# Moving the second gated unit's weights in the load order and issuing three GELU preparations at 1.25 steps a piece

## The chip, the cores and the metric

The kernel runs on one core of one Trainium2 chip. The metric is the device time of one execution in microseconds (us), the median of the runs shown. The core's engines each take their instructions in the order of the program: TensorE (PE, with its weight loads as PEld), VectorE (DVE), ScalarE (ACT), GpSimd (POOL), and SyncE (SP), which here only issues DMAs. ACT issues DMAs too, in the same order as its other instructions; the profile lists these as ACTq and those of SP as SPq.

## The reference

One layer of a bidirectional encoder over 2048 tokens of width 1024, in float32: an RMSNorm, one wide input projection, windowed attention (branch A), a state-space model (branch B), and then, which is the part that matters here:

```python
y = jax.nn.gelu(y)                                    # y: output of the state-space model
y = y * jax.nn.sigmoid(y @ w_glu + b_glu)             # the gated unit (GLU)
ssm = y * jax.nn.silu(z_ssm)
merged = jax.nn.sigmoid(g_attn) * (attn @ w_branch_attn) \
       + jax.nn.sigmoid(g_ssm) * (ssm @ w_branch_ssm)
x = x + merged @ w_out
return rms_norm(x, final_norm_gain)
```

## The kernel before

Float32 accuracy is had from pairs: each operand is split into a rounded part (a copy on ACT, names ending in h) and the rest (a subtraction, names ending in l), and each product is three matmuls: high by high, high by low, low by high.

The tokens are four blocks of 512, worked in the order 2, 3, 1, 0. Everything up to the attention is done first; beside its last projections runs a chain of side work that ends with the GELU of block 2. The final stage is then, for each block: the gated unit `glu` (four pieces of 12 matmuls), `branch` (16 pieces of 12 matmuls), and `outp` (eight groups of 24 matmuls). While `branch` of one block runs, `gelu_prep` of the next block is issued beside it; then comes the next block's `glu`, then `outp` of the first. This text calls them branches 1 to 4; branches 1 to 3 have a GELU beside them.

Instructions go out in the order of the program, written by hand. `turn()` gives each side generator a credit of half its rate, and takes one step of it for each whole credit, while the credit is above zero. In `branch` there are two turns in each piece: one in the middle of the matmuls (`mm3`, after k = 1), and one at the end, in `tick()`. The pieces, counted from 0, are (e, n) = (0,0), (1,0), (0,1), (1,1), (2,0), (2,1), (3,0), (3,1) and so on to (7,1); n = 0 is the attention side and n = 1 the state-space side. A piece issues its matmuls; then a DVE product with the gate (L1543, which frees the PSUM bank); where n = 1 also the sum `m` (DVE, L1547), its copy `mh` (ACT, L1548) and the loads of two gates (ACT's queue, L1500); then `tick()`, which issues the rest `ml` (DVE, L1556) and takes its turn; and last, where n = 0, `wahead(2)`, which splits the weights for two column blocks further: `wh` on ACT (L163), and `wl` on POOL in four quarters (L155). (After the piece (1,0) it is `wahead(1)`, and after (0,1) `wahead(2)`.)

`gelu_prep` has 16 steps. Step 1 issues the loads of the first two 128-row tiles of `yt` (ACT's queue, L1423; each reads runs of 64 floats), step 2 nothing. A tile then takes four sub-steps in four consecutive steps of a sequence that starts every third step: g0 (ACT, L1429), g1 and g2 (DVE L1433, ACT L1437), g3 with the copy `gh` (DVE L1441, ACT L1442), and g4, the rest `gl` (DVE, L1446):

```python
            for k in range(13):
                for s_ in range(3, -1, -1):
                    e, r = divmod(k - s_, 3)
                    if r == 0 and 0 <= e < 4:
                        steps[s_](e)
                yield
                if k in (4, 7):
                    ld((k - 4) // 3 + 2)
```

So step 3 has g0 of tile 0; step 8 the load of tile 2 and g3 of tile 1; step 9 g0 of tile 2; step 11 the load of tile 3 and g3 of tile 2; step 12 g0 of tile 3; steps 13 and 14 g1, g2 and then g3 of tile 3; and step 15 its `gl`.

The weights come through two buffers `raw` (512 KB each, loads on SP), in the order of the list `witems`: item j + 2 is loaded when item j is split and its buffer is free. Between the last projections and the first branch the list holds the output matrix's first half in four quarters (`wo`, split by ACT and DVE), the two `w_glu` items (the first split by ACT and DVE, the second by ACT and POOL), and then the eight items of the branch. In the last three projections of block 1, two items each are split ahead of the matmuls.

Of the kernel before, what the change touches and what calls it, by code (L numbers as in the profile page):

```python
# [37 lines left out]
def kernel(  # L38
# [89 lines left out]
    def add_side(gen, rate=1.0):  # L128
        sd = {"gen": gen, "rate": rate, "credit": 0.0, "done": False}
        sides.append(sd)  # L130
        return sd
# [4 lines left out]
    def drain(sd):  # L136
        while not sd["done"]:
            tick()
# [28 lines left out]
    witems = []  # L167
# [20 lines left out]
    def wsplit_next():  # L188
        j = wpos["split"]
        wload_to(j)  # L190
        it = witems[j]
        if it[0] == "h":
            h_split(it[1], it[2], wraw.pop(j).rearrange("p k c -> p (k c)").rearrange("p (k c) -> p k c", k=2))
        elif it[0] == "wo":
            wo_split(0, it[1], wraw.pop(j).rearrange("p k c -> p (k c)").rearrange("p (k c) -> p k c", k=2), V)
        else:
            wsplit.append(split_w(j, KD, 128, eng=V if j == wpos["glu"] else Q))
        wpos["split"] += 1
        if wpos["lag"]:
            later(wpos["lag"], lambda: wload_to(j + 2))  # L200
        else:
            wload_to(j + 2)
# [86 lines left out]
    def proj(kind, e, b, w):  # L289
        pt = bank("pj")  # L290
        mm3(pt, w, hblk[b], KD)
        evac(kind, e, b, pt)
# [953 lines left out]
    with tc.manual_schedule():  # L1246
# [3 lines left out]
        BO = (2, 3, 1, 0)  # L1250
        wo = {}
# [40 lines left out]
        for b in BO:  # L1292
            for e in (0, 2):
                if b == BO[0]:
                    witems.append(("wo", e))
                    witems.append(("wo", e + 4))
                witems.append([w_glu[0, :, (e + i) * 128:(e + i + 1) * 128] for i in range(2)])
            for e in range(KD):
                witems.append([w[0, :, e * 128:(e + 1) * 128] for w in (w_branch_attn, w_branch_ssm)])
        xp = s1.enter_context(tc.tile_pool(name="xp", bufs=1))  # L1300
# [31 lines left out]
        for b in range(NBLK):  # L1332
            gen = None
            for i, key in enumerate(wlist):
# [20 lines left out]
                if b == 0 and i == 0:  # L1355
                    sg = start(xp, wlist[0:2], wsplit1, wt)
# [47 lines left out]
        def ftile(shape, dt, tag, name, bufs=1):  # L1404
            return fin["fp"].tile(shape, dt, tag=tag, name=name, bufs=bufs)
# [9 lines left out]
        def gelu_prep(b, lag):  # L1415
            gx[b] = [ftile([128, 4, BLK], F32R, t, t) for t in ("gh", "gl")]
            gh, gl = gx[b]
            tl = {}

            def ld(e):  # L1420
                t = ftile([128, D], F32, "xr", "yt", 3)
                y = t[:, 0:BLK].rearrange("p (j m) -> p j m", j=T)
                A.dma_start(out=y, in_=yS[e * 128:(e + 1) * 128, :, b * 64:(b + 1) * 64])  # L1423
                ta = t[:, BLK:D]
                tl[e] = (y.rearrange("p j m -> p m j"), ta, ta.rearrange("p (m j) -> p m j", j=T))

            def g0(e):
                yv, ta, tav = tl[e]
                A.activation(tav, yv, AF.Square, scale=GELU_Q)  # L1429

            def g1(e):
                yv, ta, tav = tl[e]
                V.scalar_tensor_tensor(tav, tav, 1.0, yv, ALU.add, ALU.mult)  # L1433

            def g2(e):
                yv, ta, tav = tl[e]
                A.activation(ta, ta, AF.Tanh, scale=GC)  # L1437

            def g3(e):
                yv, ta, tav = tl[e]  # L1440
                V.scalar_tensor_tensor(tav, tav, 1.0, yv, ALU.add, ALU.mult)  # L1441
                A.activation(gh[:, e], ta, AF.Copy)  # L1442

            def g4(e):
                yv, ta, tav = tl.pop(e)
                V.tensor_tensor(gl[:, e], ta, gh[:, e].bitcast(F32), ALU.subtract)  # L1446

            def g12(e):
                g1(e)
                g2(e)  # L1450

            steps = (g0, g12, g3, g4)
            ld(0)
            ld(1)
            for _ in range(1 + lag):
# [10 lines that stand above are left out]
        def attn_prep(b, lag):  # L1466
            ax[b] = [ftile([128, 4, BLK], F32R, t, t) for t in ("ah", "al")]
            ah, al = ax[b]
            tok = slice(b * BLK, (b + 1) * BLK)
            ar = {}  # L1470

            def ld(e):
                ar[e] = gtile("ar")
                A.dma_start(out=ar[e], in_=aS[e * 128:(e + 1) * 128, tok])

            ld(0)
            ld(1)
            for _ in range(1 + lag):
                yield
            for e in range(4):  # L1480
                if lag:
                    yield
                r = ar.pop(e)
                A.activation(ah[:, e], r, AF.Copy)
                V.tensor_tensor(al[:, e], r, ah[:, e].bitcast(F32), ALU.subtract)
                yield
                if e + 2 < 4:
                    ld(e + 2)
# [14 lines left out]
        def glu(b):  # L1503
            gh, gl = gx.pop(b)
            sx[b] = [ftile([128, 4, BLK], F32R, t, t) for t in ("sh", "sl")]
            sh, sl = sx[b]
            for e in range(4):
                if e + 2 < 4:
                    load_zs(b, e + 2)
                if e % 2 == 0:  # L1510
                    w2 = wnext()
                w = [t[:, (e % 2) * 4:(e % 2) * 4 + 4] for t in w2]
                pt = bank("pj")
                mm3(pt, w, (gh, gl), 4)
                ta = ttile("ta")
                zs = zst.pop((b, e))
                g2 = ftile([128, BLK], F32, "g2", "g2")
                V.tensor_tensor(g2, gh[:, e].bitcast(F32), gl[:, e].bitcast(F32), ALU.add)
                A.activation(ta, pt, AF.Tanh, scale=0.25, bias=fin["bgl"][:, e:e + 1])
                V.tensor_tensor(g2, g2, zs, ALU.mult)  # L1520
                V.scalar_tensor_tensor(ta, ta, 1.0, g2, ALU.add, ALU.mult)
                A.activation(sh[:, e], ta, AF.Copy, scale=0.125)
                V.scalar_tensor_tensor(sl[:, e], ta, 0.125, sh[:, e].bitcast(F32), ALU.mult, ALU.subtract)
                if e == 2:
                    load_gt(b, 0)
                tick()
                if e < 2:
                    wahead(2 + e)
# [46 lines left out]
        def load_xr(b, t, q=None):  # L1575
            r0 = b * BLK + t * 128
            xrs[b, t] = ftile([128, D], F32, "xr", "xr", 3)
            (q or nc.sync).dma_start(out=xrs[b, t], in_=x[r0:r0 + 128, :])
# [95 lines left out]
        ws = [wnext(1), wnext(1), wnext(0)]  # L1674
        for b in (0, 1):
            for n, (key, w) in enumerate(zip(second[-3:], ws)):
                for _ in range(2 if b == 1 else 0):
                    wsplit_next()
                proj(key[0], key[1], b, w)
        drain(sd)  # L1680
# [3 lines left out]
        for i, b in enumerate(BO):  # L1684
            nxt = BO[i + 1] if i + 1 < NBLK else None
            if nxt is not None:
                sg = add_side(gelu_prep(nxt, 1), 1.0)
            branch(b, nxt)
            if nxt is not None:
                drain(sg)  # L1690
            load_xr(b, 0, A)
            if nxt is not None:
                glu(nxt)
                sa = add_side(attn_prep(nxt, 1), 1.0)
            outp(b, nxt is None)
            if nxt is not None:
                drain(sa)
# [48 lines left out]
```

## Time and profile before

| | |
|---|---|
| median of 3 runs | 1496.83 us (1495.30 to 1497.23) |
| the profiled execution's own time | 1497.58 us |
| its span, first to last instruction | 1495.8 us |
| PE busy | 1411.9 us, 94% of the span |
| DVE, ACT, POOL busy | 1042.3, 659.8, 636.9 us |
| granted TensorE clock, mean | 0.981 of full |

The final stage begins at about 1061 us of the span. A timeline row reads: start, length (both us), engine, line of the program, operation, output from input by the program's names, shapes, count; in brackets the idle time of the engine just before, and what ended it. For a DMA on ACTq or SPq the length is that of the issue alone. In a row of groups the numbers after the shapes are the count, then total busy us and the mean in ns, then the idle time before.

### The profile page before, as it was taken

Reading aid. Unit: us, or ns where it says so; the run is one execution under the profiler, and the core shown is the slowest. Engines: PE = TensorE matmul, PEld = TensorE weight load, DVE = VectorE, ACT = ScalarE, POOL = GpSimd, SP = SyncE. Lnnn points to the kernel's source line nnn. Section 1 sums busy time; section 2 is a strip of 40 time slices with the busy share of each in tenths; the row PEclk is TensorE's granted clock in tenths of the full one; section 3 lists DMA queues with packets and bytes.
Section 4 is the critical chain, followed back from the end, with each engine's and each line's share of the span. In section 5 each row is a group of like instructions: output and inputs, shape, how many; then the busy total and the mean of one; then the engine's idle time right before and its main releaser. Section 6 shows DMA issues by size and latency. Waiting matters only on the chain.

```text
span 1495.8 us, 19697 instructions
## 1 busy us (share of the span) xinstructions
PE 1411.9 (94%) x6933; PEld 1151.1 (77%) x6933; DVE 1042.3 (70%) x1954; ACT 659.8 (44%) x1213; POOL 636.9 (43%) x683
## 2 busy tenths in 40 slices
PE   7999779899999999899999999999989999999998
PEld 6787567777778777788888888888767887878886
DVE  2427977779788788656999998883678376485442
ACT  6432133433534534535666666664444243243211
POOL 5520187758688787732111111113367054153320
PEclk9999989989999999999999999999999999999999
DMA  8543222322332332455233333334676476375441
GB/s 268 156 105 90 64 81 74 99 92 71 119 106 82 116 106 82 149 170 142 86 95 93 96 95 89 99 99 141 201 210 175 140 185 184 117 186 177 129 120 70
DMA packets 240722, 185.47 MB, mean 124 GB/s; under 512 B 57920, under 2 KB 202432, under 8 KB 240624
## 3 DMA queue, kind: packets, MB, share of 16 engines
q10 hardware_dynamic: 118192, 107.89, 24.5%
q1 hardware_dynamic: 122432, 76.34, 17.1%
q8 instruction: 54, 0.88, 0.2%
q14 instruction: 44, 0.36, 0.1%
HBM read 126.56 MB, written 57.62 MB: 123 GB/s over the span
## 4 chain that ended last, share of the span: by engine, by line
PE 45%; DVE 19%; POOL 7%; DMA 6%; issue 6%; ACT 4%; ACTq 1%; POOLq 0%; DVEq 0%; SPq 0%
PE pj L221 8%; PE pj L220 8%; PE pj L222 8%; PE s L1593 4%; PE s L1592 4%; PE s L1594 4%; POOL wl L155 3%; DMA yt<-yS 2%; PE s L1163 2%; DVE Hl L891 2%; PE s L1110 2%; PE s L1147 2%; DVE pl L1152 1%; PE s L858 1%; DVE X L879 1%
## 5 line engine op out<-in xcount | busy, mean ns | idle before, releaser
L155 POOL TENSOR_TENSOR wl<-raw,wh 128x256 fp32r<-128x256 f32 x380 | 352.9, 959 | 575.1 <-ACT wh L163 443.6
L220 PE MATMUL pj<-hh,wh 128*128 128x512 f32 x976 | 390.7, 400 | 0.0
L221 PE MATMUL pj<-hl,wh 128*128 128x512 f32 x976 | 385.2, 395 | 0.0
L222 PE MATMUL pj<-hh,wl 128*128 128x512 f32 x976 | 385.1, 395 | 0.0
L222 PEld LDWEIGHTS pj<-hh,wl 128*128 128x128 f32 x976 | 185.4, 190 | 40.9
L220 PEld LDWEIGHTS pj<-hh,wh 128*128 128x128 f32 x976 | 186.1, 191 | 33.9
L221 PEld LDWEIGHTS pj<-hl,wh 128*128 128x128 f32 x976 | 185.8, 190 | 34.1
L163 ACT ACTIVATE wh<-raw 128x1024 fp32r<-128x1024 f32 x96 | 100.7, 1051 | 22.0 <-issue 4.4
L1592 PE MATMUL s<-woh,mh 128*128 128x512 f32 x256 | 101.3, 396 | 0.0
L1594 PE MATMUL s<-woh,ml 128*128 128x512 f32 x256 | 101.3, 396 | 0.0
L1593 PE MATMUL s<-wol,mh 128*128 128x512 f32 x256 | 101.3, 396 | 0.0
L1127 ACT ACTIVATE p<-p,sml 128x384 f32<-128x384 f32 (+1 forms) x128 | 75.8, 594 | 16.3 <-DVE sml L1123 16.2
L404 ACT ACTIVATE st<-pj,bg 128x512 f32<-128x512 f32 x64 | 43.8, 685 | 77.7 <-PE pj L222 71.6
L1111 DVE CUSTOM_DVE_ANT_0 p<-s,bias 128x384 f32<-128x384 f32 (+1 forms) x128 | 68.2, 534 | 14.1 <-PE s L1110 13.7
L1636 POOL TENSOR_TENSOR sm<-sm,mhalf 128x1 f32<-128x1 f32 x15 | 8.3, 551 | 160.3 <-DVE sm L1635 123.7
L867 DVE TENSOR_TENSOR rt<-X,es 128x1020 f32<-128x1020 f32 x32 | 43.3, 1353 | 38.1 <-issue 14.3
L1152 DVE TENSOR_TENSOR pl<-s,ph 128x512 fp32r<-128x512 f32 x92 | 62.8, 683 | 4.3 <-ACT ph L1150 2.9
L1110 PE MATMUL s<-kst,qs 128*128 128x384 f32 (+1 forms) x256 | 65.7, 339 | 0.0
L1599 DVE TENSOR_TENSOR xr<-xr,s 128x512 f32<-128x512 f32 x32 | 21.9, 684 | 60.0 <-PE s L1594 60.0
L870 DVE TENSOR_TENSOR X<-X,rt 128x510 f32<-128x510 f32 x64 | 62.1, 1009 | 1.1
L891 DVE TENSOR_TENSOR Hl<-X,Hh 64x1024 fp32r<-64x1024 f32 x32 | 46.1, 1440 | 17.5 <-ACT Hh L886 17.0
L1594 PEld LDWEIGHTS s<-woh,ml 128*128 128x128 f32 x256 | 48.1, 188 | 11.7
(307 smaller groups left out, 3046.1 us busy)
## 6 DMA issues: line engine op xcount, KB each, us to landing
raw<-in_w_in_dram SPq DMA_DIRECT2D x59, 512.0 KB
gS<-st ACTq DMA_DIRECT2D x64, 256.0 KB
gt<-gS ACTq DMA_DIRECT2D x64, 256.0 KB
x<-in_x_dram SPq DMA_DIRECT2D x16, 512.0 KB
raw<-in_w_branch_attn_dram SPq DMA_DIRECT2D x32, 256.0 KB
raw<-in_w_branch_ssm_dram SPq DMA_DIRECT2D x32, 256.0 KB
out_dram<-xr ACTq DMA_DIRECT2D x15, 512.0 KB
xr<-in_x_dram SPq DMA_DIRECT2D x12, 512.0 KB
```

The lines of the kernel that those rows point to most:

```text
L155: eng.tensor_tensor(lo[:, ks], r[:, ks], hi[:, ks].bitcast(F32), ALU.subtract)
L163: A.activation(res[0], r, AF.Copy)
L220: PE.matmul(pt, w[0][:, k], r[0][:, k], start=start and k == 0, stop=False)
L221: PE.matmul(pt, w[0][:, k], r[1][:, k], start=False, stop=False)
L222: PE.matmul(pt, w[1][:, k], r[0][:, k], start=False, stop=stop and k == kt - 1)
L891: V.tensor_tensor(H[1][rows], xv, H[0][rows].bitcast(F32), ALU.subtract)
L1110: PE.matmul(pt[:, 0:w], s["qs"][:, h], kst[:, r, kv, k0 * 128:k1 * 128], start=r == 0, stop=r == 1)
L1127: A.activation(p[:, h, 0:w], p[:, h, 0:w], AF.Exp, bias=nm[:, j:j + 1], accum_out=den[:, j:j + 1])
L1152: return lambda: V.tensor_tensor(pl, pt, ph.bitcast(F32), ALU.subtract)
L1592: PE.matmul(pt, mh[k][:, ts_], wo[0, n][:, k], start=k == 0, stop=False)
L1593: PE.matmul(pt, mh[k][:, ts_], wo[1, n][:, k], start=False, stop=False)
L1594: PE.matmul(pt, ml[k][:, ts_], wo[0, n][:, k], start=False, stop=k == KD - 1)
```

## The change

Two edits. The last quarter of the output matrix's first half (`wo` 6) moves behind the second `w_glu` item in the list, and the last projection of block 1 splits one item ahead of its matmuls where it split two; so `wo` 6 is split at the end of the first `glu` piece, ahead of the first branch item. And the side generator of the later GELUs gets a rate of 1.25 where it had 1.0: five steps in eight turns in place of four.

```diff
             for e in (0, 2):
                 if b == BO[0]:
                     witems.append(("wo", e))
-                    witems.append(("wo", e + 4))
+                    if e == 0:
+                        witems.append(("wo", 4))
                 witems.append([w_glu[0, :, (e + i) * 128:(e + i + 1) * 128] for i in range(2)])
+                if b == BO[0] and e == 2:
+                    witems.append(("wo", 6))
...
             for n, (key, w) in enumerate(zip(second[-3:], ws)):
-                for _ in range(2 if b == 1 else 0):
+                for _ in range((2, 2, 1)[n] if b == 1 else 0):
                     wsplit_next()
                 proj(key[0], key[1], b, w)
...
             if nxt is not None:
-                sg = add_side(gelu_prep(nxt, 1), 1.0)
+                sg = add_side(gelu_prep(nxt, 1), 1.25)
             branch(b, nxt)
```

## Rows read from the trace of the kernel before

**Rows 1.** Timeline of PE: the gated-unit waits behind branches 1, 2 and 3.
```profile
1137.32 0.50 PE L221 MATMUL pj<-gl,wh 128*128 128x512 f32 x1 [2.10 <-DVE gl L1446]
...
1241.55 0.50 PE L221 MATMUL pj<-gl,wh 128*128 128x512 f32 x1 [1.54 <-DVE gl L1446]
...
1345.53 0.50 PE L221 MATMUL pj<-gl,wh 128*128 128x512 f32 x1 [1.57 <-DVE gl L1446]
```

**Rows 2.** Windows: length, busy of PE, PEld, DVE, ACT, POOL, then clock, DMA.
```profile
1191.00:1235.90 44.90, 44.90 (x194) 35.84 (x192) 32.03 (x38) 19.43 (x25) 22.35 (x25) 1.00 0.74 176
...
1071.00:1074.00 3.00, 3.00 (x9) 2.33 (x8) 2.00 (x3) 2.21 (x4) 1.78 (x3) 0.50 0.76 263
```

**Rows 3.** Timeline of ACT and its DMA queue (ACTq) in branch 2.
```profile
1193.05 0.53 ACTq L1423 DMA_DIRECT2D yt<-yS  x1
...
1194.35 1.06 ACT L163 ACTIVATE wh<-raw 128x1024 fp32r<-128x1024 f32 x1 [1.05 <-issue]
1198.44 1.14 ACT L1429 ACTIVATE yt<-yt 128x512 f32<-128x512 f32 x1 [3.04 <-DMA yt<-yS]
...
1215.12 0.53 ACTq L1423 DMA_DIRECT2D yt<-yS  x1
...
1219.66 1.16 ACT L1429 ACTIVATE yt<-yt 128x512 f32<-128x512 f32 x1 [0.41 <-DMA yt<-yS]
...
1224.53 0.81 ACTq L1500 DMA_DIRECT2D gt<-gS  x2
1225.38 0.53 ACTq L1423 DMA_DIRECT2D yt<-yS  x1
...
1232.00 1.13 ACT L1429 ACTIVATE yt<-yt 128x512 f32<-128x512 f32 x1 [2.98 <-DMA yt<-yS]
```

**Rows 4.** Groups by line in branch 2: count, busy us, mean ns, idle.
```profile
L1556 DVE SCALAR_TENSOR_TENSOR ml<-m,mh 128x512 fp32r<-128x512 f32 x8 | 8.3, 1032 | 8.3 <-ACT mh L1548 8.3
L1547 DVE TENSOR_TENSOR m<-gt 128x512 f32<-128x512 f32 x8 | 7.9, 987 | 0.3
...
L1543 DVE SCALAR_TENSOR_TENSOR gt<-gt,s 128x512 f32<-128x512 f32 x8 | 5.4, 678 | 0.9 <-PE s L222 0.9
L1433 DVE SCALAR_TENSOR_TENSOR yt<-yt 128x512 f32<-128x512 f32 x4 | 4.9, 1224 | 0.0
L1441 DVE SCALAR_TENSOR_TENSOR yt<-yt 128x512 f32<-128x512 f32 x4 | 4.9, 1222 | 0.2
L1446 DVE TENSOR_TENSOR gl<-yt,gh 128x512 fp32r<-128x512 f32 x4 | 2.7, 685 | 0.3 <-ACT gh L1442 0.3
...
L1548 ACT ACTIVATE mh<-m 128x512 fp32r<-128x512 f32 x8 | 5.1, 632 | 8.9 <-DVE m L1547 8.9
...
L1437 ACT ACTIVATE yt<-yt 128x512 f32<-128x512 f32 x4 | 2.5, 634 | 5.4 <-DVE yt L1433 5.4
L1442 ACT ACTIVATE gh<-yt 128x512 fp32r<-128x512 f32 x4 | 2.5, 632 | 5.5 <-DMA gt<-gS 2.8 <-DVE yt L1441 2.7
```

**Rows 5.** Timeline of ACT: the first `yt` step of branches 1 and 3.
```profile
1093.65 1.14 ACT L1429 ACTIVATE yt<-yt 128x512 f32<-128x512 f32 x1 [5.28 <-DMA yt<-yS]
...
1302.84 1.14 ACT L1429 ACTIVATE yt<-yt 128x512 f32<-128x512 f32 x1 [3.19 <-DMA yt<-yS]
```

**Rows 6.** Timeline of the first gated unit; the DMA row is the chain's.
```profile
1066.11 1.06 ACT L1274 ACTIVATE woh<-raw 128x1024 fp32r<-128x1024 f32 x1 [2.46 <-DMA raw<-in_w_out_dram]
...
1068.46 0.37 SPq L183 DMA_DIRECT2D raw<-in_w_branch_attn_dram  x1
1068.73 0.67 ACT L404 ACTIVATE st<-pj,bg 128x512 f32<-128x512 f32 x1
...
1068.90 3.70 POOL L155 TENSOR_TENSOR wl<-raw,wh 128x256 fp32r<-128x256 f32 x4 [27.41 <-ACT wh L163]
...
1073.05 4.78 DMA raw<-in_w_branch_ssm_dram
...
1073.65 0.67 ACT L1519 ACTIVATE ta<-pj,bgl 128x512 f32<-128x512 f32 x1
```

## The prediction

> **What bounds the kernel now.** I read the waits of PE first, then the timeline of PE, ACT and DVE through the final stage, then groups by line for the prices. PE is the bound: in branch 2 it is busy in all 44.9 us at full clock [rows 2], which makes 44.9 / 16 = 2.8 us a piece. Its waits come where the next block's gated unit begins: the eleventh matmul of its first piece waits for `gl` of the GELU's last tile, 2.10, 1.54 and 1.57 us behind branches 1, 2 and 3 [rows 1]. The rows of branch 3 stand 104.0 us behind those of branch 2 [rows 1]; 20 pieces of 2.8 and eight groups of 24 matmuls of 2.8 / 12 each make 100.8, so a round holds some 3.2 us of waits, and no change of the GELU's order can win more there. Ten matmuls are 2.33 us, so without that last wait each gated unit would have begun at 1135.0, 1239.2 and 1343.2. I compare these three marks, because behind them PE runs on.
>
> The reader is to see a second thing: ACT, in program order, stands still at g0 until `yt` has landed, 3.04 us for tile 0 and 2.98 us for tile 3 [rows 3]. From issue to the step it took 5.39 us (tile 0), 4.54 (tile 2) and 6.62 (tile 3) [rows 3]. Whatever lies behind g0 on ACT waits too.
>
> **The change, the GELU's rate.** Credits rise by 0.625 a turn instead of 0.5. With m for a piece's middle and e for its end, steps 1 to 15 stood at m0, m1, ... m14. Now they stand at m0, e0, e1, m2, m3, m4, e4, e5, m6, m7, m8, e8, e9, m10, m11. No instruction is added or removed; the order on ACT and DVE changes, and with it what is behind a wait:
>
> - g0 of tile 0 (step 3) was behind the weight split `wh` for piece 4 (1194.35, then 1198.44) [rows 3]; at e1 it comes ahead of it.
> - g0 of tile 2 (step 9) moves from m8 to m6, ahead of the split for piece 10; its load (step 8) is now half a piece ahead of it, not a whole one, and only a `gh` lies between them on ACT.
> - g0 of tile 3 (step 12) moves from m11 to e8, ahead of the split for piece 12, again half a piece behind its load.
> - `gh` of tile 3 (step 14) moves to m10, ahead of the split for piece 14.
>
> So three loads that used to hold up little now stand before the weights that PE needs next. The question is whether the GELU's chain runs faster when it is issued earlier. Its prices, by means of groups and by single durations [rows 3, 4]: g1 and g3 1.22 each, product 0.68, `m` 0.99, `ml` 1.03, `gl` 0.69, `mh`, g2 and `gh` 0.63 each, g0 1.14, `wh` 1.06, a pair of gate loads 0.81.
>
> From the end of g0 of tile 0 to the load of tile 2, DVE has now two g1, one g3, one `gl`, four products (pieces 2 to 5), three `m`, two `ml`, and waits for three `mh`; ACT then issues a pair of gate loads: 2.44 + 1.22 + 0.69 + 2.72 + 2.97 + 2.06 + 1.89 + 0.81 = 14.8 us. The same arithmetic on the old order (one more `ml`, no gate pair) gives 15.0, and the rows show 1215.12 - 1199.58 = 15.5. So the load goes out hardly earlier: DVE sets this, not the place in the program.
>
> The load itself: bounds 4.54 and 6.62. I take 5.4, the row of tile 0, which like both loads now follows directly on a pair of gate loads.
>
> From there to the load of tile 3: g0 1.14, g1 1.22, product 0.68, `m` 0.99, `mh` 0.63, gates 0.81 = 5.5 (the rows show 5.7 in the old order, 1219.66 to 1225.38). Its load: 5.4 again.
>
> From its landing, on ACT and DVE in turn: g0 1.14, split for piece 12 1.06, `mh` 0.63, `ml` 1.03, g1 1.22, g2 0.63, g3 1.22, `gh` 0.63, split for piece 14 1.06 = 8.6. Then POOL's first quarter of `wl`, 3.70 / 4 = 0.93 [rows 6], less two matmuls, 0.45; then pieces 14 and 15, 5.6; in all 14.7 to the gated unit. What was late at its start, `gl`, is now there before PE asks for it; late instead are the weights of pieces 10, 12 and 14.
>
> Sum from the end of g0 of tile 0: 14.8 + 5.4 + 5.5 + 5.4 + 14.7 = 45.8. Branch 2: 1199.6 + 45.8 = 1245.4 against 1239.2, 6.2 us late. Branch 3: 1302.84 + 1.14 [rows 5] + 45.8 = 1349.8 against 1343.2, 6.6 late. Branch 1 begins at 1093.65 + 1.14 = 1094.8 [rows 5] and has two more 128x512 copies of output weights (0.63 each) in that chain on ACT: 1141.9 against 1135.0, 6.9 late, to which comes what the first edit adds. There PE also stands at piece 4, whose split waits for the load of tile 0; that is the same chain and is not counted twice. Nor does DVE's idle time cover anything: PE waits for ACT.
>
> The Trainium skill (DMA: Bandwidth & Descriptors, the SWDGE section on the anatomy of one DMA) prices a transfer at about 2.0 us and its bytes over 436 GB/s, for these 256 KB an estimate of 2.6 us; by it both loads would come 5.6 us sooner, and a branch would be about as long as before. The rows of this kernel show 4.54 at the least, for runs of 256 bytes beside other traffic and on another path, and they decide.
>
> **The change, the weights' order.** Ahead of the first gated unit, ACT splits `wo` 6 at 1066.11, the second GLU item next, and only then evacuates the last projection at 1068.73, for whose PSUM bank PE's third piece waits [rows 6]. With one split less, and its load one place earlier, this evacuation comes at about 1066.11 + 1.06 - 0.1 = 1067.1, so 1.7 us sooner (bounds 0 and 1.7), and POOL's `wl` too. But the first branch item's load, issued at 1068.46 when DVE had emptied `wo` 6's buffer, now waits for POOL to empty the GLU item's: 1068.90 - 1.7 + 3.70 = 1070.9. It lands 4.78 us later [rows 6], at 1075.7, and its split (1.06) stands on ACT ahead of the second GLU piece's tanh, which moves from 1073.65 to 1076.7 [rows 6]. The `wo` 6 split itself, one ACT and one DVE instruction, falls into that wait and costs nothing; if the load came sooner, it would cost up to its 1.06. Of these 3.0 us late part is taken back by waits that the old order has there: bounds 0 and 3.0; I take 1.2, since the products on DVE are then done ahead. PE gains 1.7 at the third piece and gives it back standing before the branch's first.
>
> **Sum.** 6.9 + 1.2 + 6.2 + 6.6 = 20.9. The profiled execution took 1497.6 (span 1495.8 and 1.8 around it), 0.7 above the median of the runs; so 1496.8 + 20.9 = 1517.7, and I say 1517.
>
> **Rivals.**
>
> *Faster: the GELU is done early and its waits go.* For it: `gl` is the named releaser at all three marks. Then PE wins 2.10 + 1.54 + 1.57 = 5.2, and up to 1.7 before the third piece of the first gated unit: 1490. Against it: the split for piece 14 is behind step 14 on ACT. It decides when tile 3 lands before 1239.2 - 14.7 = 1224.5 in branch 2; my chain has 1230.7, the old rows 1232.0; the two loads would have to take 4.6 us together, where the quickest one in the rows, twice, makes 9.1.
>
> *No change.* The new waits inside the branch equal the old ones behind it, because the loads are quicker when they are issued in a quieter stretch; near the 2.6 us each above, or with shorter DVE steps: 1495 to 1500.
>
> *Slower, and the clock falls.* After the wait before the first gated unit's third piece the granted clock was 0.50 for some 3 us [rows 2], which is 1.2 of 2.4 GHz; my chain has PE standing still for 3 and then 5 us in branch 2 (the splits for pieces 10 and 12 end at 1199.6 + 14.8 + 5.4 + 2.2 = 1222.0 and at 1232.9; without waits the pieces would begin at 1191.0 + 28 = 1219.0 and, 3.0 us late, at 1227.6). If every branch loses 2 us so, 1523. In part this is hidden, as PE then waits for weights anyway. The Trainium skill (TensorE: Matmul & The Clock Gate, Why this matters for your kernels) says that idle gaps between bursts of matmuls bring the half clock back; after the 2.10 us wait [rows 1] the rows show full clock, so this does not always happen.
>
> *The second edit does nothing that can be seen, the first costs or wins 1 to 2 us*: 1495 to 1499, counted with no change.
>
> **How the numbers follow.** A difference of 0.2%, 3.0 us, is about what a measurement of this kernel can tell. My forecast has 0.52, its clock variant 0.19, no change 0.12, faster 0.17. So slower 0.71, same 0.12, faster 0.17. The forecast's own range: both loads at 4.54 take 1.7 a branch off, DVE's steps without contention about 1 more, the first edit at 0 takes 1.2: 1508; at 6.62 they add 2.4 a branch, the first edit at 3.0 adds 1.8: 1526. To hold 8 in 10 the range goes down to the edge of no change, 1498, and ends at 1525.
>
> **What would show it.** In the profile after, on ACT in branch 2: g0 of tile 0 at about 1198 with `wh` behind it; the load of tile 2 within a microsecond of 14.8 us after that step's end; PE idle in front of pieces 10 and 12, released by `wh` (L163) or `wl`, some 3 and 5 us; no wait for `gl` at the gated unit; in the first gated unit the third piece sooner, and then a wait of some 4 us before the first branch piece. Wrong it is if PE runs through pieces 8 to 15 without waits: then ACT was ahead of PE by more than the rows let me see, or the loads landed in under 4 us.

## The result, and the profile after

The changed kernel takes 1524.14 us (median of 4 runs, 1523.96 to 1525.46), the kernel before 1497.03 beside it (4 runs); the ratio is 1.0182, 95% interval 1.0164 to 1.0200. The forecast was 1517, slower, with a range from 1498 to 1525, so the time lies in the range, 0.9 us below its upper end. The profiled execution after has a span of 1523.5 us (1495.8 before), PE busy for 1426.1 us, and a mean granted clock of 0.972 (0.981 before).

I read PE's waits first. The view groups them by line, for 1050 to 1400 us: total us, times, longest.

```profile
PE pj L220 <- ACT wh L163: 19.6, 9, 5.0
PE pj L220 <- ACT ta L1522: 2.9, 1, 2.9
PE pj L222 <- POOL wl L155: 2.8, 3, 1.4
PE pj L220 <- ACT st L404: 2.3, 2, 1.4
```

The releaser `gl` of [rows 1] is gone altogether, and `wh`, the split of weights on ACT, has taken its place: 19.6 us in nine waits. The kernel before has 3.3 in three there:

```profile
PE pj L220 <- ACT wh L163: 3.3, 3, 1.6
```

The timeline of PE after says in front of which pieces the long waits are: the first of branch 1 (1081.13, released by `ta`), its pieces 4 and 10, and pieces 10 and 12 of branches 2 and 3, all released by `wh`.

```profile
1081.13 0.51 PE L220 MATMUL pj<-ah,wh 128*128 128x512 f32 x1 [2.88 <-ACT ta L1522]
...
1101.02 0.80 PE L220 MATMUL pj<-ah,wh 128*128 128x512 f32 x1 [4.96 <-ACT wh L163]
...
1122.74 0.50 PE L220 MATMUL pj<-ah,wh 128*128 128x512 f32 x1 [2.04 <-ACT wh L163]
...
1235.71 0.50 PE L220 MATMUL pj<-ah,wh 128*128 128x512 f32 x1 [2.14 <-ACT wh L163]
...
1247.15 0.80 PE L220 MATMUL pj<-ah,wh 128*128 128x512 f32 x1 [3.80 <-ACT wh L163]
1247.74 0.63 PE L221 MATMUL pj<-al,wh 128*128 128x512 f32 x1
1248.17 0.63 PE L222 MATMUL pj<-ah,wl 128*128 128x512 f32 x1
...
1347.92 0.50 PE L220 MATMUL pj<-ah,wh 128*128 128x512 f32 x1 [2.25 <-ACT wh L163]
...
1357.80 0.50 PE L220 MATMUL pj<-ah,wh 128*128 128x512 f32 x1 [2.13 <-ACT wh L163]
```

Why `wh` is late stands on ACT and its queue. This is the timeline after of branch 1's beginning, then of branch 2; [rows 3] is the same place before.

```profile
1091.97 1.24 ACTq L1426 DMA_DIRECT2D yt<-yS  x2
1098.95 1.06 ACT L1432 ACTIVATE yt<-yt 128x512 f32<-128x512 f32 x1 [7.21 <-DMA yt<-yS]
1099.92 1.04 ACT L163 ACTIVATE wh<-raw 128x1024 fp32r<-128x1024 f32 x1
...
1152.41 0.63 ACT L1274 ACTIVATE woh<-wor 128x512 fp32r<-128x512 f32 x1 [6.53 <-DMA wor<-in_w_out_dram]
...
1212.73 1.14 ACT L1432 ACTIVATE yt<-yt 128x512 f32<-128x512 f32 x1 [5.23 <-DMA yt<-yS]
1213.77 1.05 ACT L163 ACTIVATE wh<-raw 128x1024 fp32r<-128x1024 f32 x1
...
1227.96 0.53 ACTq L1426 DMA_DIRECT2D yt<-yS  x1
...
1233.65 1.06 ACT L1432 ACTIVATE yt<-yt 128x512 f32<-128x512 f32 x1 [2.71 <-DMA yt<-yS]
1234.62 1.04 ACT L163 ACTIVATE wh<-raw 128x1024 fp32r<-128x1024 f32 x1
...
1238.60 0.53 ACTq L1426 DMA_DIRECT2D yt<-yS  x1
...
1245.09 1.06 ACT L1432 ACTIVATE yt<-yt 128x512 f32<-128x512 f32 x1 [3.82 <-DMA yt<-yS]
1246.06 1.04 ACT L163 ACTIVATE wh<-raw 128x1024 fp32r<-128x1024 f32 x1
```

Each split stands right behind a g0 that has waited for its load, and PE's first matmul of the piece begins when the split ends (1247.15 against 1246.06 + 1.04). The windows view shows what such a wait leaves behind; the last three numbers of a row are clock, DMA share and GB/s. In pieces 12 of branches 2 and 3 the clock is 0.50 (1.2 of 2.4 GHz) and 0.64, and at 0.50 one matmul follows the other after 0.43 us (1247.74, 1248.17) in place of 0.23; in the first nine pieces of branch 2, with no wait, it is 1.00.

```profile
1205.29:1230.60 25.31, 25.31 (x109) 20.18 (x108) 17.22 (x20) 10.41 (x14) 10.49 (x12) 1.00 0.65 161
...
1247.15:1252.40 5.25, 5.25 (x12) 4.06 (x13) 4.05 (x4) 1.29 (x3) 4.08 (x4) 0.50 0.32 82
...
1357.80:1362.60 4.80, 4.72 (x12) 3.46 (x13) 3.60 (x3) 1.10 (x2) 4.09 (x4) 0.64 0.31 76
```

Where the 27.7 us of span lie, by PE's timeline (a branch is counted from its first matmul to the first of the output groups, so with the next gated unit; without a wait that is 56.0 us):

| stretch | before | after | more |
|---|---|---|---|
| to the first gated unit | 1061.35 | 1063.56 | 2.2 |
| first gated unit | 15.34 | 17.57 | 2.2 |
| branch 1 | 69.60 | 79.37 | 9.8 |
| branch 2 | 59.44 | 67.15 | 7.7 |
| branch 3 | 59.16 | 64.96 | 5.8 |
| the rest (output groups, branch 4) | 230.9 | 230.9 | 0.0 |

### The profile page after: what moved, and what is told of

Read it like the earlier page. It is cut to its first block, busy times and chain, and to the rows that moved or that the text cites. A ratio compares the mean times of both kernels' runs of the same rounds, so it can differ in the third digit from the quotient of the medians.

```text
span 1523.5 us, 19708 instructions
## 1 busy us (share of the span) xinstructions
PE 1426.1 (94%) x6933; PEld 1160.0 (76%) x6933; DVE 1043.8 (69%) x1954; ACT 659.2 (43%) x1213; POOL 639.8 (42%) x683
## 3 DMA queue, kind: packets, MB, share of 16 engines
q1 hardware_dynamic: 122432, 76.34, 16.8%
## 5 line engine op out<-in xcount | busy, mean ns | idle before, releaser
L163 ACT ACTIVATE wh<-raw 128x1024 fp32r<-128x1024 f32 x96 | 100.6, 1050 | 26.0 <-DMA zs<-zsS 5.6
L1111 DVE CUSTOM_DVE_ANT_0 p<-s,bias 128x384 f32<-128x384 f32 (+1 forms) x128 | 68.3, 534 | 14.1 <-PE s L1110 13.8
L404 ACT ACTIVATE st<-pj,bg 128x512 f32<-128x512 f32 x64 | 43.8, 685 | 77.9 <-PE pj L222 68.2
L220 PE MATMUL pj<-ah,wh 128*128 128x512 f32 x128 | 56.6, 442 | 21.6 <-ACT wh L163 18.7
L1152 DVE TENSOR_TENSOR pl<-s,ph 128x512 fp32r<-128x512 f32 x92 | 62.9, 683 | 4.3 <-ACT ph L1150 2.9
L222 PE MATMUL pj<-ah,wl 128*128 128x512 f32 x128 | 56.9, 445 | 2.7 <-POOL wl L155 2.3
```

The lines of the kernel that those rows point to most:

```text
L163: A.activation(res[0], r, AF.Copy)
L220: PE.matmul(pt, w[0][:, k], r[0][:, k], start=start and k == 0, stop=False)
L222: PE.matmul(pt, w[1][:, k], r[0][:, k], start=False, stop=stop and k == kt - 1)
L1111: V.tensor_tensor_reduce(out=p[:, h, 0:w], in0=pt[:, 0:w], in1=bias[:, kv * 4 + h, r0:r1:-1], scale=1.0, scalar=0.0, op0=ALU.add, op1=ALU. ...
L1152: return lambda: V.tensor_tensor(pl, pt, ph.bitcast(F32), ALU.subtract)
```

## The experiments

There are twelve kernels, each timed against the kernel before. The table has the profile's durations, cut as above, and the ratio of the times with its 95% interval; what each kernel is, stands below. The start of the first gated unit lies between 1061.0 and 1063.6 in all the profiles, and in the ten kernels that leave the code up to there as it was before, the unit itself takes between 12.5 and 17.0 us: these two stretches differ from one execution to the next by as much as the change seemed to cost there.

| kernel | first unit | branch 1 | 2 | 3 | ratio |
|---|---|---|---|---|---|
| before | 15.3 | 69.6 | 59.4 | 59.2 | |
| after | 17.6 | 79.4 | 67.2 | 65.0 | 1.0182 (1.0164 to 1.0200) |
| e1_order | 14.7 | 69.7 | 59.1 | 59.2 | 1.0010 (0.9996 to 1.0023) |
| e2_rate | 12.8 | 80.0 | 66.4 | 64.6 | 1.0154 (1.0134 to 1.0175) |
| e3_wfirst | 14.9 | 76.6 | 63.2 | 65.4 | 1.0135 (1.0115 to 1.0156) |
| e4_early | 17.0 | 79.7 | 62.9 | 62.9 | 1.0123 (1.0102 to 1.0143) |
| e10_wstart | 12.7 | 78.9 | 61.1 | 61.0 | 1.0104 (1.0087 to 1.0122) |
| e7_four | 15.9 | 77.9 | 63.4 | 63.5 | 1.0099 (1.0083 to 1.0115) |
| e9_back | 13.7 | 80.2 | 60.3 | 60.5 | 1.0079 (1.0065 to 1.0093) |
| e11_late | 12.5 | 70.2 | 64.9 | 64.2 | 1.0080 (1.0062 to 1.0097) |
| e13_old_loads | 13.0 | 70.8 | 57.8 | 57.7 | 0.9982 (0.9971 to 0.9994) |
| e14_rate_all | 15.7 | 79.4 | 58.1 | 58.2 | 1.0048 (1.0032 to 1.0063) |
| e15_old_all | 15.9 | 78.3 | 56.7 | 57.3 | 1.0014 (0.9998 to 1.0029) |
| e16_first_loads | 16.8 | 75.9 | 57.8 | 57.8 | 1.0032 (1.0018 to 1.0045) |

**e1_order: the first edit alone.**

```diff
-                sg = add_side(gelu_prep(nxt, 1), 1.25)
+                sg = add_side(gelu_prep(nxt, 1), 1.0)
```

> Only the weights' order is changed; the GELU's rate stays 1.0. Theory A (the two edits add up, and this one costs what the first gated unit lost): the first gated unit takes 17.6 us from its first piece to the branch's first instead of 15.3, the branches behind it stand as in the kernel before, with their waits for gl; about 1499 us, 2.2 over the kernel before. Rival B (the first branch's loss belongs to this edit too, because its first weights and the last quarter of the output matrix come later): branch 1 loses several us more, 1503 to 1507. Rival C (the loss in the first gated unit came with the two us by which that profile was late already): no difference within 0.2%, 1495 to 1499.

Measured 1500.12 against 1498.37 us (12 and 17 runs). The branches are those of the kernel before, so rival B is out. The time alone does not decide between theory A, whose 2.2 us would be a ratio of 1.0015, and rival C: the interval takes in both. The profile speaks for C, with 14.7 us for the unit where theory A has 17.6. In the timeline of PE the unit has the shape that the forecast gave it: its third piece begins 6.1 us after the first (8.1 before), and 2.8 us are given back ahead of the branch.

```profile
1068.47 0.50 PE L220 MATMUL pj<-gh,wh 128*128 128x512 f32 x1 [0.36 <-ACT st L404]
...
1077.08 0.50 PE L220 MATMUL pj<-ah,wh 128*128 128x512 f32 x1 [2.76 <-ACT ta L1522]
```

**e2_rate: the second edit alone.** From here on all kernels have the old weights' order.

```diff
-                sg = add_side(gelu_prep(nxt, 1), 1.0)
+                sg = add_side(gelu_prep(nxt, 1), 1.25)
```

> Only the GELU's rate is changed; the weights' order is the one before. Theory A (the weights of pieces 10 and 12 stand on ACT behind g0's waits for yt): branches 2 and 3 lose 7.7 and 5.8 us as in the kernel after, branch 1 some 7 to 10; PE waits for wh in each and never for gl: 1518 to 1521. Rival B (a good part of branch 1's loss comes from the weights' order): branch 1 loses under 5 us, 1512 to 1516.

Measured 1519.93, ratio 1.0154: theory A. Branches 1, 2 and 3 lose 10.4, 7.0 and 5.4 us against the kernel before, 22.8 together, with PE waiting 20.6 us for `wh` and never for `gl`. The rate is the loss, in branch 1 too.

**e3_wfirst: the splits ahead of the GELU's step.**

```diff
+                if (e, n) == (1, 0):
+                    wahead(1)
+                elif (e, n) == (0, 1) or e >= 2 and n == 0:
+                    wahead(2)
                 tick()
...
-                if (e, n) == (1, 0):
-                    wahead(1)
-                elif (e, n) == (0, 1) or e >= 2 and n == 0:
-                    wahead(2)
```

> The rate alone is changed, as in e2_rate, but in the branches the next weights are split ahead of the GELU's step instead of behind it. Theory A (the loss is the place of wh behind g0's wait): PE's waits for wh at pieces 4, 10 and 12 go, and since the GELU still ends before the gated unit asks for gl, the kernel is no slower than before: 1488 to 1497. Rival B (DVE and ACT are simply given too much ahead of the branch's end, so that products and mh come late wherever wh stands): PE waits for banks or for ta instead, 1508 to 1520. Rival C (only the half clock after the waits is lost): between, 1500 to 1508.

Measured 1518.00, which is in rival B's range: theory A's number is missed by over 20 us. But the edit did not do all that I took it to do. The split for piece 10 goes out at the end of piece 6, and g0 of tile 2 in the middle of piece 6, so it still stands behind; the waits at piece 4 and for g0 of tile 3 at piece 12 were moved, that one was not, and a new one came at piece 14 (1.48 us in branch 2, 2.80 in branch 3). Timeline of ACT in branch 2, and PE's piece 10:

```profile
1227.35 1.06 ACT L1429 ACTIVATE yt<-yt 128x512 f32<-128x512 f32 x1 [4.17 <-DMA yt<-yS]
1228.32 1.04 ACT L163 ACTIVATE wh<-raw 128x1024 fp32r<-128x1024 f32 x1
```
```profile
1229.41 0.50 PE L220 MATMUL pj<-ah,wh 128*128 128x512 f32 x1 [2.94 <-ACT wh L163]
```

**e4_early: the loads three steps earlier.**

```diff
-                if k in (4, 7):
-                    ld((k - 4) // 3 + 2)
+                ks = (4, 7) if b in BO[:2] else (1, 4)
+                if k in ks:
+                    ld(ks.index(k) + 2)
```

> The rate alone is changed, as in e2_rate, but in branches 2 and 3 the loads of yt tiles 2 and 3 are issued three of the GELU's steps earlier (branch 1 keeps its loads). Theory A (the distance from a load to its step is what is short): g0 of tiles 2 and 3 no longer waits there (2.7 and 3.8 us in branch 2, 2.8 and 2.3 in branch 3 in the kernel after), PE runs through pieces 10 and 12 at full clock, and the two branches take about 57 and 57 us to the end of the gated unit, less than before; with branch 1's loss kept: 1500 to 1507. Rival B (DVE's steps set the pace, the loads were only the last to be seen): ACT's waits go over to waits for DVE at g2 and gh, and the branches stay over 62 us: 1512 to 1520.

Measured 1518.40, the branches at 62.9: by its numbers rival B. g0 of tiles 2 and 3 does not wait any more, and half of the loss in branch 2 is still there: ACT now stands still earlier, at the issue of tile 2's load, whose buffer the store of the last output tile (1217.51) still holds. Timeline of ACT and its queue:

```profile
1217.51 0.44 ACTq L1643 DMA_DIRECT2D out_dram<-xr  x1
...
1223.59 0.53 ACTq L1423 DMA_DIRECT2D yt<-yS  x1
1224.21 0.63 ACT L1442 ACTIVATE gh<-yt 128x512 fp32r<-128x512 f32 x1 [5.15 <-DMA raw<-in_w_branch_attn_dram]
```

The bracket names the transfer whose signal came last before `gh`. What held the load itself is in the trace's signals: the store has landed at 1223.49, and ACT's wait for it ends at 1223.51. In branch 2 ACT waits for DVE too, as rival B says, by 2.4 us at the most at one time. So neither of the two runs decides; the next four do.

**e10_wstart: the splits at the start of the pieces**, on e2_rate.

```diff
                 if n == 0:
                     ws[e] = wnext(0)
+                    if e >= 2:
+                        wahead(2)
```

with the two calls for the first pieces ahead of `tick()`, as in e3_wfirst.

> Rate 1.25 as in e2_rate (old weights' order); each branch weight is now split at the start of the piece that e3_wfirst split it behind, so that on ACT the splits for pieces 10, 12 and 14 stand ahead of g0 of tile 2, g0 of tile 3 and gh of tile 3. Theory A (PE waits only for a split that stands behind a g0 waiting for its load; in e3_wfirst the one for piece 10 still did): no wait for wh of pieces 10 and 12 in branches 2 and 3, which take about 57 to 59 us to the end of the gated unit: 1490 to 1500. Rival B (the chain of ACT and DVE itself is later, and with it mh, ml and the products): PE waits for a bank or for wl instead, the branches stay above 61 us: 1508 to 1520.

Measured 1514.12. In branches 2 and 3 the loss falls from 7.0 and 5.4 us to 1.7 and 1.8, although g0 of tiles 2 and 3 still waits (2.53 and 2.66 us in branch 2): the waits cost little when the split that PE needs next is not behind them. The wait that is left in branch 2, 2.32 us, is at piece 14, whose split (1241.05) still stands behind g0 of tile 3 (1237.14). The branches (61.1 and 61.0) miss theory A's 57 to 59, and the time as a whole misses it too, because branch 1 keeps 78.9; by its numbers this is rival B.

**e7_four: a fourth buffer**, on e4_early. The kernel leaves out the final gain, and the buffer takes its place; each row is multiplied by itself instead.

```diff
-                t = ftile([128, D], F32, "xr", "yt", 3)
+                t = ftile([128, D], F32, "xr", "yt", 4)
...
-                V.scalar_tensor_tensor(xr, xr, sm[:, 1:2], fin["fg"], ALU.mult, ALU.mult)
+                V.scalar_tensor_tensor(xr, xr, sm[:, 1:2], xr, ALU.mult, ALU.mult)
```

> Rate 1.25 and the early loads of e4_early, with a fourth buffer for the tiles, so that the load of tile 2 no longer waits for the last output tile's store (5.2 us of ACT in e4_early). The space is the final gain's: the gain is left out, each row of the result is multiplied by itself instead, with the same instruction. Theory A (it is the waiting for the loads on ACT): in branches 2 and 3 g0 of tiles 2 and 3 does not wait, PE waits under 1 us a branch; they take 56 to 59 us to the end of the gated unit, branch 1 keeps its 80: 1503 to 1508. Rival B (DVE's steps set the pace): as e4_early, 62 to 63 us each, 1514 to 1518.

Measured 1512.96, between the two ranges, with the branches at 63.4: by their length rival B, by the rows neither. ACT again stands still, 4.59 us, now ahead of g0 of tile 1, until a load of weights has landed that this g0 does not read:

```profile
1214.36 0.38 SPq L183 DMA_DIRECT2D raw<-in_w_branch_attn_dram  x1
...
1220.91 2.06 ACTq L1499 DMA_DIRECT2D gt<-gS  x2
1223.02 1.12 ACT L1427 ACTIVATE yt<-yt 128x512 f32<-128x512 f32 x1 [4.59 <-DMA raw<-in_w_branch_ssm_dram]
```

The instructions in the trace say why: the transfers of both queues use eight completion counters by turns, and an issue waits until the transfer that had its counter before has landed. The gate load at 1220.91 has the counter of the weight load that SP issued at 1214.36 and that landed at 1220.89. A load put early moves the turns of those behind it; that this is what brought the two together was not tried.

**e9_back: the loads one and two steps earlier**, with the three buffers, on e2_rate: `ks = (4, 7) if b in BO[:2] else (3, 5)`.

> Rate 1.25; in branches 2 and 3 the load of tile 2 goes out one of the GELU's steps earlier and that of tile 3 two steps, with the three buffers there are. Theory A: the load of tile 2 still waits a little for the last output tile's store and g0 of tile 2 for up to 2 us, g0 of tile 3 not at all; the branches take 59 to 62 us, between e2_rate and e7_four: 1508 to 1513. Rival B (DVE sets the pace): no gain over e2_rate, 1518 to 1521.

Measured 1510.16, and the branches at 60.3 and 60.5: theory A. With less of the issue's own waiting than e7_four it is the quicker one, which speaks against DVE as what sets the pace. What is left in branch 2 are waits for `wh` of 1.37 and 0.78 us at pieces 12 and 14, and there ACT waits for DVE (2.27 us for g3 at 1233.06).

**e11_late: the old rate, the loads a step later**: `ks = (4, 7) if b in BO[:2] else (5, 8)`.

> The GELU's old rate 1.0, but in branches 2 and 3 the loads of tiles 2 and 3 one step later, directly ahead of their g0. No step of the GELU's arithmetic moves. Theory A (the distance from the load to its g0 is what was lost, the rate only took it away): g0 of tile 2 waits some 5 us and that of tile 3 some 5, and PE waits for wh as in the kernel after; each of the two branches loses 4 to 8 us: 1505 to 1513. Rival B (the loss comes from DVE's steps being early): within 0.3% of the kernel before, 1496 to 1501.

Measured 1511.20, ratio 1.0080: theory A. Branches 2 and 3 lose 5.4 and 5.0 us without any change of rate. Timeline of ACT in branch 2, then PE's piece 12: the picture is of the same kind as in the kernel after, only that at this rate it is the split for piece 12 that stands behind g0 of tile 2.

```profile
1218.52 0.53 ACTq L1423 DMA_DIRECT2D yt<-yS  x1
1224.79 1.06 ACT L1429 ACTIVATE yt<-yt 128x512 f32<-128x512 f32 x1 [6.49 <-DMA yt<-yS]
1225.76 1.04 ACT L163 ACTIVATE wh<-raw 128x1024 fp32r<-128x1024 f32 x1
```
```profile
1226.85 0.50 PE L220 MATMUL pj<-ah,wh 128*128 128x512 f32 x1 [2.86 <-ACT wh L163]
```

**e13_old_loads: the kernel before with e9_back's loads**, rate 1.0.

> The kernel before with its rate 1.0; only the loads of yt tiles 2 and 3 go out one and two of the GELU's steps earlier in branches 2 and 3, as in e9_back. Theory A (also in the kernel before the end of the GELU is late by the 2.98 us that g0 of tile 3 waits for its load): the waits for gl, and the 1.0 and 0.7 us for wh ahead of them, go in branches 2 and 3, which take 56.9 us to the end of the gated unit instead of 59.4 and 59.2: 1492 to 1495. Rival B (the steps on DVE bring gl late in any case): the waits for gl stay over 1 us, 1496 to 1500.

Measured 1496.16 against 1499.31 (12 and 27 runs), ratio 0.9982, which is 2.7 us: faster than both kernels. The branches are full (44.8 us for 16 pieces), so the waits for `wh` are gone; but `gl` is waited for as long as before, 1.50 us, as rival B said, and the time is in its range. The timeline of DVE, and of PE's eleventh matmul, shows why: `gl` of tile 3 stands behind the branch's last `ml`, which waits for the `mh` of PE's last piece. Counted from the branch's start `gl` comes 1.7 us sooner than before, but PE asks for it 1.6 us sooner, and the wait stays.

```profile
1237.85 1.14 DVE L1557 SCALAR_TENSOR_TENSOR ml<-m,mh 128x512 fp32r<-128x512 f32 x1 [0.70 <-ACT mh L1549]
1238.91 0.68 DVE L1446 TENSOR_TENSOR gl<-yt,gh 128x512 fp32r<-128x512 f32 x1
```
```profile
1239.64 0.50 PE L221 MATMUL pj<-gl,wh 128*128 128x512 f32 x1 [1.50 <-DVE gl L1446]
```

**e14_rate_all: rate 1.25 with both remedies**, `ks = (3, 6)` in branch 1 and `(3, 5)` in branches 2 and 3, and the splits of e10_wstart.

> Rate 1.25 in all three branches with everything found so far turned back: the splits at the start of the pieces as in e10_wstart, the earlier loads of e9_back, and in branch 1 both loads one step earlier. Theory A (what the rate costs is its loads' distance and the place of the splits): branches 2 and 3 take 57 to 59 us to the end of the gated unit, branch 1 74 to 77: 1498 to 1504, at most 0.4% over the kernel before. Rival B (at this rate DVE hands its results on too late anyway): branches 2 and 3 above 60, branch 1 at 78 to 80: 1506 to 1512.

Measured 1507.12. Branches 2 and 3 take 58.1 and 58.2 us, 1.3 and 1.0 less than before the change: there the two remedies give back more than the rate costs, as theory A says. Branch 1 stays at 79.4, as rival B says, and the total with it.

**e15_old_all: the same at rate 1.0.**

> The kernel before with its rate 1.0, with the splits and the loads of e14_rate_all. Theory A: no wait for gl or wh in branches 2 and 3, and in branch 1 the 1.6 us for wh and the 2.1 for gl go: 1489 to 1494. Rival B (at rate 1.0 the splits stand ahead of the g0 steps already, so moving them wins nothing): as e13_old_loads, within 2 us.

Measured 1500.86, which neither theory has. Branches 2 and 3 are the shortest of all (56.7 and 57.3), 1.4 and 0.9 us shorter than in e14_rate_all: with the same splits and loads the higher rate still costs something and wins nothing. Branch 1 is at 78.3, with the old rate, so moving the splits and loads costs some 8 us there by itself. In e10_wstart and e14_rate_all branch 1 can therefore not be read for what the rate does.

The trace shows what else moved in branch 1. The output weights' second half comes there in four loads (`wor`) on SP, which ACT splits (`woh`). Waits of ACT from 1075 to 1160 us, before and in e15_old_all:

```profile
ACT woh L1274 <- DMA wor<-in_w_out_dram: 0.6, 2, 0.3
```
```profile
ACT woh L1274 <- DMA wor<-in_w_out_dram: 16.0, 3, 5.7
```

SP issues in the order of the program. A split put ahead brings the next weights' load ahead of the `wor` load, and that weights' load waits until POOL has emptied its buffer (1112.15 in e15_old_all). SP's timeline around the second `wor` load, before and in e15_old_all; counted from the branch's start the load goes out at 28.0 and at 34.3 us:

```profile
1104.64 0.37 SPq L1254 DMA_DIRECT2D wor<-in_w_out_dram  x1
...
1108.34 0.37 SPq L183 DMA_DIRECT2D raw<-in_w_branch_attn_dram  x1
```
```profile
1112.17 0.37 SPq L183 DMA_DIRECT2D raw<-in_w_branch_attn_dram  x1
...
1113.19 0.44 SPq L1254 DMA_DIRECT2D wor<-in_w_out_dram  x1
```

In the same stretch of e3_wfirst, e10_wstart and e14_rate_all these waits add up to 11.2, 13.3 and 14.6 us. No run issues the `wor` loads earlier, so how much of the 8 us hangs on them is not shown.

**e16_first_loads: the first loads of branch 1 ahead of the first gated unit**, branch 1 at rate 1.25, the others as e13_old_loads.

```diff
+        g1st = gelu_prep(BO[1], 1)
+        next(g1st)
...
+        def first_gelu():
+            yield
+            yield from g1st
...
         glu(BO[0])
...
-                sg = add_side(gelu_prep(nxt, 1), 1.0)
+                sg = add_side(first_gelu() if i == 0 else gelu_prep(nxt, 1), 1.25 if i == 0 else 1.0)
```

> Branch 1 alone at rate 1.25, with its first two yt loads issued ahead of the first gated unit instead of at the branch's start; branches 2 and 3 as in e13_old_loads. Theory A (branch 1's ten us come from g0 of tile 0, which waits 7.6 us for its load there and holds the split for piece 4 behind it): g0 of tile 0 does not wait, PE does not stand at piece 4, and all that hangs on it comes some 7 us sooner: branch 1 takes 72 to 75 us to the end of the gated unit instead of 80.0, and the kernel 1496 to 1500. Rival B (in branch 1 POOL, which has the low parts of the output weights beside those of the branch's, or DVE holds PE up at this rate anyway): branch 1 stays at 77 or more, 1501 to 1506.

Measured 1504.74, in rival B's range (with 16.8 us for the first unit, which now has these loads in it). Branch 1 takes 75.9, between the two theories: g0 of tile 0 no longer waits, PE's wait at piece 4 is gone, and 4.1 of the 10.4 us come back. On ACT and DVE:

```profile
1090.25 1.11 ACT L1428 ACTIVATE yt<-yt 128x512 f32<-128x512 f32 x1 [0.41 <-issue]
1091.26 1.04 ACT L163 ACTIVATE wh<-raw 128x1024 fp32r<-128x1024 f32 x1
```
```profile
1095.08 0.69 DVE L1545 SCALAR_TENSOR_TENSOR gt<-gt,pj 128x512 f32<-128x512 f32 x1 [3.91 <-PE s L221]
1095.68 1.09 DVE L1432 SCALAR_TENSOR_TENSOR yt<-yt 128x512 f32<-128x512 f32 x1
```

Counted from the branch's start g0 of the tile begins 8 us sooner than in e2_rate, but g1 on DVE stands behind the product of a piece that PE has not finished. Later in the branch the loads of tiles 2 and 3 are waited for as in e2_rate (2.34 and 2.74 us), and PE for `wh` at pieces 10, 12 and 14 (3.00, 1.09 and 1.11).

## Why the prediction was right, point by point

The sign, the cause and the chain were right: ACT, in order, stops at g0 until `yt` has landed, and the weights that PE needs next are behind it. Its links, from the end of g0 of tile 0, against the rows after:

| link | forecast | branch 1 | 2 | 3 |
|---|---|---|---|---|
| to the load of tile 2 | 14.8 | 15.7 | 14.1 | 14.1 |
| its load | 5.4 | 4.4 | 5.7 | 5.8 |
| to the load of tile 3 | 5.5 | 5.3 | 5.0 | 4.4 |
| its load | 5.4 | 5.5 | 6.5 | 5.5 |
| to the gated unit | 14.7 | 16.4 | 16.2 | 15.3 |
| sum | 45.8 (branch 1: 47.1) | 47.3 | 47.4 | 45.0 |

- **The chain's end is the term that was too small**: 15.3 to 16.4 in place of 14.7. In branch 2, from PE's last wait (piece 12, 1247.15) to the gated unit (1261.25) four pieces take 14.1 us instead of 11.2; in branch 3, from 1357.80 to 1371.00, 13.2. These 2.9 and 2.0 us are the half clock behind the wait. In part they hide the last wait of the forecast, at piece 14: in branch 2 its split ends 8.7 us after g0 began (forecast 8.6), but PE, slowed, comes later than that and does not wait. So the end is longer by 1.5 and 0.6 us. The clock rival (2 us a branch, 1523) had the mechanism right, but its price is more than this. In branch 1 the last wait is at piece 14, with no half clock behind it.
- **That the time came near the clock rival's 1523 is in good part chance.** The profile is 6.8 us above the sum of 20.9. Of these, 2.2 lie ahead of the first gated unit and 1.0 in it, 2.9 in branch 1, and only 0.7 in branches 2 and 3 together.
- **A wait that the sum did not have**: behind branch 1 the gated unit itself takes 13.2 us, 2.0 more than its 11.2. ACT stands there 6.53 us for the last load of the output weights' second half (1152.41), with a split behind it. That is the larger part of branch 1's 9.8 against 6.9. The kernels at rate 1.25 with the splits in their old place all have this wait, 6.1 to 6.7 us from 1075 to 1162 us; those at rate 1.0 with the splits there have 0.6 to 2.4.
- **The weights' order, 1.2 us in the sum**, cannot be measured: e1_order has 1.0010 with an interval that takes in 1. The 2.2 us that the profile after has there, like the 2.2 ahead of it, are within what executions differ by. The two edits alone cost 0.10% and 1.54%, together 1.82%; whether there is anything in the difference, the intervals leave open. Of the two effects that cancel in the forecast both are in e1_order's rows.
- **Rivals.** *Faster* fell on the condition that it named: in branch 2 tile 3 would have had to land by 1238.7 (its 1224.5 and the 14.2 us by which the branch now begins later), and it lands at 1245.1. *No change* fell with the loads, which took 4.4 to 6.5 us. The estimate of 2.6 us from the Trainium skill (DMA: Bandwidth & Descriptors, the SWDGE section on the anatomy of one DMA) is met by none of them; the measurement decides.
- **What the forecast did not see** is that two things have to come together. In branch 2 the rate costs 7.0 us; with the loads earlier 0.9 are left (e9_back), with the splits moved ahead 1.7 (e10_wstart), and with both the branch is 1.3 shorter than before the change (e14_rate_all; at the old rate with both it is 2.8 shorter, e15_old_all). The two savings, 6.1 and 5.3, are together more than the loss, so each of them removes mostly the same wait; and a later load at the old rate makes the same loss, 5.4 (e11_late). The forecast had the load's latency as a term of a chain that DVE starts; the runs show it as the distance from the load's issue to its g0 in ACT's order, which half a piece more or less decides.
- **Also wrong in part** is the reading of [rows 1] as something to be won. e13_old_loads takes away the 2.98 us that g0 of tile 3 waits [rows 3], and the wait for `gl` stays at 1.50; what went were the waits for `wh` ahead of it.

Open in part is branch 1. Its first load explains 4.1 of 10.4 us; the loads of tiles 2 and 3 with the splits behind them, the half clock, and ACT's wait for `wor` are in the rows of the rest, but no run takes them away there without another change that costs as much (e14_rate_all, e15_old_all). That the moved splits cost 8 us there because the `wor` loads come late is read from the trace, and not tried.

## What to carry to other kernels

On an engine that works in order, a step that waits for a load has the price of what stands behind it; before steps are issued faster, look at how far each is from the load that feeds it, and at what would be next in line when it waits. Moving a load earlier is the cheap remedy (1 and 2 steps gave back 6 of 7 us, and 0.18% on the old kernel), as long as the issue itself does not have to wait for a buffer or a counter. Moving other work ahead on one engine can push a load back on another queue: look there too. And a wait that a profile names, here `gl`, may be the last of several in a row: taking away what seems to cause it may move nothing.

## What the runs showed of the hardware, and of the program on it

- A short wait of PE is mostly followed by the half clock, but not always: behind 2.14, 2.25 and 3.80 us (after) and 2.32 us (e10_wstart, branch 2) 6 to 12 matmuls of the piece ran at the lower level (0.43 us from one to the next), behind 2.76 us (e7_four) and 2.86 us (e11_late) none did, nor behind 1.37 and 0.78 us (e9_back). From 1060 to 1400 us the fourteen profiles have 48 waits of PE of 2 us or more: behind 39 of them at least four of the next 16 matmuls came 0.38 to 0.5 us after one another, behind nine at most one did.
- The load of one `yt` tile (256 KB in runs of 256 bytes) took from 4.4 to 6.5 us within one profile, from its issue to the step that waited for it, and 7.0 where both first tiles were asked for beside the output weights.
- Queues that share nothing else are tied through completion counters: ACT stood 4.59 us for transfers of SP's that it has no use for (e7_four).
